# Seven products for eight in six of the eleven pairs of the last down product

## The chip, the cores and the metric

The kernel runs on one core of a Trainium2 chip. The metric is the device time of one execution in microseconds (us). Before the change it is 992.38 us, the median of three runs from 992.32 to 992.44. The core's engines are named as in the profile: PE is the matrix engine (PEld its loads of the stationary operand), DVE the vector engine, ACT the scalar engine, POOL the GpSimd engine, and SP the queue that issues the transfers from memory.

## The reference

The model has two layers on 256 tokens of width 1024, in float32. Each layer is a half-step of a gated feed-forward block, an attention, and a second such half-step; a norm closes the whole. The change touches only the last half-step of layer 1, and of that only the product with `w_down`:

```python
def swiglu(h, w_gate, w_up, w_down):
    return (jax.nn.silu(h @ w_gate) * (h @ w_up)) @ w_down

h = h + FFN_RESIDUAL_WEIGHT * swiglu(rmsnorm(h, ffn2_norm[layer]),
                                     ffn2_w_gate[layer], ffn2_w_up[layer], ffn2_w_down[layer])
...
return rmsnorm(h, final_norm)
```

The feed-forward width is 2816, so the last product multiplies act, 256 by 2816, with weights of 2816 by 1024. `FFN_RESIDUAL_WEIGHT` is 0.5.

## The kernel before

Every product in float32 is made of three matmuls in the rounded type `float32r`: each operand x is split into a high part xh (its rounding, made by ACT) and a low part xl = x - xh (made by DVE), and the product is xh wh + xh wl + xl wh. `product` (L179) issues these three matmuls for each accumulator in PSUM that it is given. The weights come in raw units of 1 MB: `unit` (L139) lets SP load one into a buffer of the ring "raw" (four buffers), and `pieces_of` (L146) splits it in pieces of 128 by 1024: ACT writes the piece's high part (L153), DVE its low part (L154). High and low parts have rings of eight buffers each, "wh" and "wl".

The last half-step runs in two stages.

**Gate and up** (`ffn_blocks`, L340). The 22 blocks f of 128 hidden columns are taken in pairs; a pair needs a raw unit of `w_gate` and one of `w_up`, eight pieces of splits in all counting both parts. `both` (L344) makes the matmuls of a block: high parts against the 512 columns of x's two parts (L193), then low parts against 256 columns (L196). `close` (L350) turns the two accumulators of a block into a block of act, with hidden columns on the partitions and the 256 tokens in the free dimension: ACT and DVE join the two halves (L336, L337), DVE scales gate (L352), ACT applies silu (L353), POOL scales up (L355), DVE multiplies (L356), and `parts_of` (L86) splits the result (ACT L94, DVE L90). All 22 blocks of act stay in SBUF.

**Last product** (`down_last`, L408). First the residual stream is transposed back to tokens on partitions (L685, L686). Then the product takes eleven units of `w_down`, each with the rows of two blocks k and all 1024 columns. For the first 18 blocks k it issues, for each of the two halves of tokens t, three matmuls for each accumulator of that half; the last four blocks are held back, and their products are issued accumulator by accumulator, so that the eviction of one (L431), the sum of squares (L698) and the final gain (L702) run beside the matmuls of the next. The accumulators are not all of one width:

```python
segs = [[(0, 0, 512), (1, 0, 512)], [(0, 0, 512), (1, 0, 256), (1, 256, 256)]]
...
if k < nk - tail:
    for t in range(NT):
        product(accs[t], *blocks[t][k], cols(t, ws), k == 0, False)
```

PSUM has eight buffers of 128 by 512: five of tag "acc" and three of tag "tr"; the last product uses the five.

Each engine works through a queue whose order is fixed when the program is built. That order is not the order of the text: the framework moves an instruction ahead of earlier ones that still wait. The profile shows splits of `w_down` (L153 on wh_f_d) on ACT at 905.55, among the closes of blocks that stand before them in the text. An instruction that writes a buffer of a ring waits until the last reader of that buffer is done.

Of the kernel before, what the change touches and what calls it, by code (L numbers as in the profile page):

```python
# [10 lines left out]
F32 = mybir.dt.float32  # L11
F32R = mybir.dt.float32r
# [3 lines left out]
P = 128  # L16
# [9 lines left out]
NG = H // HG  # L26
ROT = 16
HALF = ROT // 2
LEAD = 4
EPS = 1e-6  # L30
SCALE = DH ** -0.5
# [31 lines left out]
def trunk(ctx: ExitStack, tc: tile.TileContext, a: dict, out: bass.AP):  # L63
# [273 lines left out]
        nc.vector.tensor_add(s, ac[:, :S], s)  # L337
        return s

    def ffn_blocks(name, wg, wu, norm, first=None, beside=()):  # L340

        blocks = []

        def both(f, pair):  # L344
            acs = [acc(f"{name}_{n}{f}") for n in "gu"]
            cols = slice(f % 2 * P, (f % 2 + 1) * P)
            products_t(acs, [[(wh[:, cols], wl[:, cols]) for wh, wl in w] for w in pair], norm.x, True, True)
            return acs

        def close(f, gate, up):  # L350
            g = joined(gate, f"{name}_g{f}")
            nc.vector.tensor_mul(g, g, norm.row)  # L352
            nc.scalar.activation(g, g, AF.Silu)  # L353
            u = joined(up, f"{name}_u{f}")
            nc.gpsimd.tensor_tensor(u, u, norm.row, op=ALU.mult)  # L355
            nc.vector.tensor_mul(g, g, u)  # L356
# [48 lines left out]
        down_t(name, wd, blocks, after)  # L405


    def down_last(name, w, nk, blocks, h, weight, part, after, tail=4):  # L408


        segs = [[(0, 0, 512), (1, 0, 512)], [(0, 0, 512), (1, 0, 256), (1, 256, 256)]]
        accs = [[acc(f"dn_{name}_{t}_{c}_{o}")[:, :n] for c, o, n in segs[t]] for t in range(NT)]
        held = []

        def cols(t, ws):
            return [tuple(w[:, c * 512 + o:c * 512 + o + n] for w in ws) for c, o, n in segs[t]]

        for u in range(nk // 2):
            for i, ws in enumerate(unit(f"{name}_{u}", 2, D, [(None, rows(w, 2 * u, 2, 0, D))])):
                k = 2 * u + i  # L420
                if k < nk - tail:
                    for t in range(NT):
                        product(accs[t], *blocks[t][k], cols(t, ws), k == 0, False)
                else:
                    held.append((k, ws))
        for t in range(NT):
            for i, (c, o, n) in enumerate(segs[t]):
                for k, ws in held:
                    product(accs[t][i:i + 1], *blocks[t][k], cols(t, ws)[i:i + 1], False, k == nk - 1)
                hc = h[t][c][:, o:o + n]  # L430
                nc.vector.scalar_tensor_tensor(hc, accs[t][i], weight, hc, op0=ALU.mult, op1=ALU.add)  # L431
                part(t, slice(c * 512 + o, c * 512 + o + n))
            after(t)

    def out_t(name, pieces, base, blocks, norm, tail=3):
# [242 lines left out]
    blocks = ffn_blocks("f21", a["ffn2_w_gate"][1], a["ffn2_w_up"][1], n6)  # L678
# [25 lines left out]
    def finish(t):  # L704
# [11 lines left out]
    down_last("f21_d", a["ffn2_w_down"][1], KF,  # L716
              [[tuple(x[:, i, t * P:(t + 1) * P] for i in range(2)) for x in blocks] for t in range(NT)],
              h, 0.5, finish_part, finish)


_INS = ["ffn1_w_gate", "ffn1_w_up", "ffn1_w_down", "ffn2_w_gate", "ffn2_w_up", "ffn2_w_down",
# [23 lines left out]
```

## Time and profile before

| what | value |
| --- | --- |
| median of three runs | 992.38 us |
| the profiled execution, its own time | 992.2 us |
| its span, first to last instruction | 990.4 us |
| granted clock of PE, mean | 0.999 |
| PE busy | 979.6 us (99% of the span) |
| DVE busy | 731.3 us (74%) |
| ACT busy | 589.2 us (59%) |
| POOL busy | 163.6 us (17%) |
| gate and up of the last half-step, one pair of blocks | 11.13 us |
| last product, first to last matmul | 922.79 to 984.10 us |

In rows of the timeline the columns are start in us, length in us, engine, line, operation, output <- inputs, shapes, and the count of instructions merged in the row; brackets give the idle time of the engine before it and what ended it. Matmuls overlap, so the pace of a run of them is read from the distance of their starts. The same holds for DVE, where an instruction starts some 0.08 us before the one ahead of it is recorded as done.

### The profile page before, as it was taken

To read this page: it belongs to the slowest core of one execution; us is meant where nothing else is said; L and a number is where in the kernel's file an instruction comes from. 1 tells how busy PE (TensorE), PEld (TensorE's weight loads), DVE (VectorE), ACT (ScalarE), POOL (GpSimd) and SP (SyncE) were. 2 spreads that over 40 slices of the span, in tenths; PEclk is the share of its full clock that TensorE was granted. 3 is DMA by queue.
4 is the path that set the end of the run, shared out by engine and by line. 5 is a ranking of instruction groups with operands and counts; after the bars stand their busy time and mean duration, and the time that the engine had idled before them with its cause. 6 is when DMAs were issued, how large, how long until landed. Compare 5 with 4: busy or idle time off the path is not lost. (4 is left out here: it accounts for less than half of the span.)

```text
span 990.4 us, 15816 instructions
## 1 busy us (share of the span) xinstructions
PE 979.6 (99%) x5949; PEld 866.1 (87%) x5949; DVE 731.3 (74%) x1284; ACT 589.2 (59%) x1084; POOL 163.6 (17%) x195
## 2 busy tenths in 40 slices
PE   9999999999999999999999999999999999999997
PEld 6888888888899888888888888888889998888886
DVE  7988866667787887776678878666687778888542
ACT  6756554467776656645455666544676766655531
POOL 3211101122202211111021111111222032111000
PEclk9999999999999999999999999999999999999999
DMA  9876565654444466556646664666534445565511
GB/s 306 259 251 200 167 225 172 209 179 144 139 129 146 153 211 187 188 192 197 200 146 203 190 202 149 216 197 203 170 129 128 129 146 176 190 182 201 211 45 43
DMA packets 158398, 176.08 MB, mean 178 GB/s; under 512 B 3568, under 2 KB 152304, under 8 KB 158320
## 3 DMA queue, kind: packets, MB, share of 16 engines
q1 hardware_dynamic: 157888, 174.50, 54.8%
q8 instruction: 47, 0.77, 0.3%
q10 hardware_dynamic: 432, 0.55, 0.2%
q14 instruction: 31, 0.25, 0.1%
HBM read 173.99 MB, written 1.05 MB: 177 GB/s over the span
## 5 line engine op out<-in xcount | busy, mean ns | idle before, releaser
L193 PE MATMUL f_g<-x_n,wh_f_g 128*128 128x512 f32 x688 | 180.0, 394 | 0.0
L193 PE MATMUL f_u<-x_n,wh_f_u 128*128 128x512 f32 x688 | 177.6, 390 | 0.0
L193 PEld LDWEIGHTS f_u<-x_n,wh_f_u 128*128 128x128 f32 x688 | 129.0, 188 | 27.2
L193 PEld LDWEIGHTS f_g<-x_n,wh_f_g 128*128 128x128 f32 x688 | 124.1, 189 | 22.7
L355 POOL TENSOR_TENSOR j_f_u<-j_f_u,r_n 128x256 f32<-128x256 f32 x88 | 77.3, 880 | 378.1 <-DVE j_f_u L337 361.1
L193 PE MATMUL dn_f<-act_f,wh_f 128*128 128x512 f32 x528 | 126.5, 391 | 0.0
L154 DVE TENSOR_TENSOR wl_f_u<-raw_f_u,wh_f_u 128x1024 fp32r<-128x1024 f32 x86 | 120.8, 1406 | 1.8 <-ACT wh_f_u L153 1.7
L154 DVE TENSOR_TENSOR wl_f_g<-raw_f_g,wh_f_g 128x1024 fp32r<-128x1024 f32 x86 | 102.9, 1225 | 17.7 <-PE f_g L196 12.0
L193 PEld LDWEIGHTS dn_f<-act_f,wh_f 128*128 128x128 f32 x528 | 96.8, 188 | 18.6
L154 DVE TENSOR_TENSOR wl_f<-raw_f,wh_f 128x1024 fp32r<-128x1024 f32 x72 | 81.8, 1153 | 36.0 <-ACT wh_f L153 26.8
L196 PE MATMUL f_u<-x_n,wl_f_u 128*128 128x256 f32 x688 | 103.3, 283 | 0.0
L196 PE MATMUL f_g<-x_n,wl_f_g 128*128 128x256 f32 x688 | 102.7, 282 | 0.0
L196 PEld LDWEIGHTS f_g<-x_n,wl_f_g 128*128 128x128 f32 x688 | 96.4, 190 | 6.3
L153 ACT ACTIVATE wh_f_g<-raw_f_g 128x1024 fp32r<-128x1024 f32 x86 | 89.4, 1049 | 13.4 <-issue 6.0
L153 ACT ACTIVATE wh_f<-raw_f 128x1024 fp32r<-128x1024 f32 x72 | 67.3, 979 | 49.5 <-PE dn_f L193 30.3
L153 ACT ACTIVATE wh_f_u<-raw_f_u 128x1024 fp32r<-128x1024 f32 x86 | 86.6, 1047 | 15.7 <-PE f_g L193 10.9
L196 PEld LDWEIGHTS f_u<-x_n,wl_f_u 128*128 128x128 f32 x688 | 91.7, 192 | 0.1
L230 POOL TENSOR_TENSOR ss_n<-ss_n,sq_n 128x256 f32<-128x256 f32 x42 | 41.7, 992 | 246.5 <-ACT sq_n L229 245.6
L94 ACT ACTIVATE act_f<-j_f_g 128x256 fp32r<-128x256 f32 x88 | 36.5, 417 | 73.2 <-DVE j_f_g L356 73.1
L353 ACT ACTIVATE j_f_g<-j_f_g 128x256 f32<-128x256 f32 x88 | 36.7, 417 | 62.5 <-DVE j_f_g L352 62.1
L196 PEld LDWEIGHTS dn_f<-act_f,wl_f 128*128 128x128 f32 x528 | 68.1, 191 | 2.8
L196 PE MATMUL dn_f<-act_f,wl_f 128*128 128x256 f32 x528 | 69.0, 283 | 0.0
(213 smaller groups left out, 1798.1 us busy)
## 6 DMA issues: line engine op xcount, KB each, us to landing
raw_f_g<-in_ffn_w_gate_dram SPq DMA_DIRECT2D x43, 1024.0 KB, 5.4
raw_f_u<-in_ffn_w_up_dram SPq DMA_DIRECT2D x43, 1024.0 KB, 5.4
raw_f<-in_ffn_w_down_dram SPq DMA_DIRECT2D x24, 1024.0 KB, 5.0
raw_f_d<-in_ffn_w_down_dram SPq DMA_DIRECT2D x11, 1024.0 KB, 4.9
raw_f<-in_ffn_w_down_dram SPq DMA_DIRECT2D x12, 768.0 KB, 4.4
raw_qka<-in_a_w_qkv_dram SPq DMA_DIRECT2D x16, 512.0 KB, 4.6
raw_kvb<-in_kv_w_dram SPq DMA_DIRECT2D x12, 512.0 KB, 4.2
raw_va<-in_a_w_qkv_dram SPq DMA_DIRECT2D x4, 1024.0 KB, 5.0
```

What stands on the lines that cost most here:

```text
L94: nc.scalar.activation(hi, src, AF.Copy, scale=scale)
L153: nc.scalar.activation(wh, r, AF.Copy)
L154: nc.vector.tensor_sub(wl, r, wh.bitcast(F32))
L193: nc.tensor.matmul(ac, wh, flat(x), start=first and i == 0, stop=False)
L196: nc.tensor.matmul(ac[:, :S], wl, x[:, 0, :], start=False, stop=last and i == len(ws) - 1)
L230: nc.gpsimd.tensor_tensor(self.ss, self.ss, sq, op=ALU.add)
L353: nc.scalar.activation(g, g, AF.Silu)
L355: nc.gpsimd.tensor_tensor(u, u, norm.row, op=ALU.mult)
```

## The change

The eleven units of the last product are now called pairs 0 to 10 (two blocks k each). For the pairs in `FAST`, which are 0, 1, 3, 5, 7 and 8, the product of act's 2 by 2 quarters (token half by block) with the weights' 2 by 2 quarters (block by column half) is made in Strassen's manner, in Winograd's form: seven products of quarters where eight stood. Four sums of quarters of act and four sums of quarters of the weights are needed for it. Three products go straight into the accumulators of the results 11, 12 and 21; the other four go into accumulators m1, m5, m6 and m7 or on to 21, are added up over all six pairs, and are combined once, by `collect`, into the residual stream.

- The sums of act are made in the gate and up stage by `quarter_sums`, called from `close` of the odd block of a fast pair: four POOL instructions of 128 by 128 in a chain, then two splits of 128 by 256 (ACT and DVE). They stay in buffers that the attention used before.
- The sums of the weights are made in the last product by `load`: one DVE addition of 128 by 1024 and two POOL additions of 128 by 512 in a chain, into a second buffer of the ring "raw". A fast pair then has seven quarters to split instead of four: three pieces of 128 by 1024 and one of 128 by 512 on ACT and on DVE, in place of two of 128 by 1024.
- Pairs 2, 4 and 6 keep their eight products, the last two pairs (four blocks, as before) are held back. All accumulators are now 512 wide; the last one of the held work is cut in two halves, the second in a PSUM buffer of its own. Eight PSUM buffers are used in place of five.
- The matmuls of one accumulator are issued three in a row, where before those of two or three accumulators alternated.

```diff
+    def quarter_sums(a, b, hi, lo, name):
+        c, d = etile(f"qc_{name}"), etile(f"qd_{name}")
+        a0, a1, b0, b1 = a[:, :P], a[:, P:], b[:, :P], b[:, P:]
+        for out, x, y, op in ((c[:, :P], b1, a1, ALU.subtract), (c[:, P:], a0, a1, ALU.subtract),
+                              (d[:, :P], c[:, :P], a0, ALU.add), (d[:, P:], b0, d[:, :P], ALU.subtract)):
+            nc.gpsimd.tensor_tensor(out, x, y, op=op)
+        parts_of(hi[:, :S], lo[:, :S], c)
+        parts_of(hi[:, S:], lo[:, S:], d)
...
             parts_of(x[:, 0], x[:, 1], g)
+            if sums is not None and f // 2 in sums:
+                if f % 2 == 0:
+                    held[f // 2] = g
+                else:
+                    quarter_sums(held.pop(f // 2), g, *sums[f // 2], f"{name}_{f}")
...
+        c11, c12, c21, m1, m5 = [acc(f"dn_{name}_{n}") for n in ("11", "12", "21", "m1", "m5")]
+        c22, m6, m7 = [trt(f"dn_{name}_{n}") for n in ("22", "m6", "m7")]
...
+        def load(i):
+            raw = rawp.tile([P, 4, 512], F32, tag="raw", name=f"raw_{name}_{i}")
+            nc.sync.dma_start(raw.rearrange("p (k c) n -> p k (c n)", k=2), rows(w, 2 * i, 2, 0, D))
+            if i not in sums:
+                return split(raw[:, :2], f"{i}a") + split(raw[:, 2:], f"{i}b")
+            t = rawp.tile([P, 4, 512], F32, tag="raw", name=f"sum_{name}_{i}")
+            nc.vector.tensor_add(t[:, :2], raw[:, 0::3], raw[:, 1:2].to_broadcast([P, 2, 512]))
+            nc.gpsimd.tensor_tensor(t[:, 2], t[:, 0], raw[:, 3], op=ALU.add)
+            nc.gpsimd.tensor_tensor(t[:, 3], t[:, 2], raw[:, 2], op=ALU.add)
+            b11, b21 = split(raw[:, 0::2], f"{i}a")
+            b22, = split(raw[:, 3:], f"{i}b")
+            ta, tc = split(t[:, :2], f"{i}c")
+            tb, td = split(t[:, 2:], f"{i}d")
+            return b11, b21, b22, ta, tc, tb, td
...
+            for n, ac, left, right in (("1", m1, x[0][0], b11), ("11", c11, x[0][1], b21), ("12", c12, l3, b22),
+                                       ("5", m5, l5, ta), ("7", m7, l7, tc), ("6", m6, l6, tb),
+                                       ("21", c21, x[1][1], td)):
+                add(n, ac, left, right, last and len(n) == 1)
...
+        def collect():
+            a, b, c, d = [atile([P, 512], name=f"co_{name}_{n}") for n in "abcd"]
+            nc.scalar.activation(a, m1, AF.Copy, scale=weight)
+            nc.vector.scalar_tensor_tensor(b, m6, weight, a, op0=ALU.mult, op1=ALU.subtract)
+            nc.gpsimd.tensor_tensor(h[0][0], h[0][0], a, op=ALU.add)
+            nc.vector.scalar_tensor_tensor(c, m7, weight, b, op0=ALU.mult, op1=ALU.subtract)
+            nc.vector.scalar_tensor_tensor(b, m5, -weight, b, op0=ALU.mult, op1=ALU.add)
+            nc.gpsimd.tensor_tensor(h[0][1], h[0][1], b, op=ALU.add)
+            nc.vector.scalar_tensor_tensor(d, m5, -weight, c, op0=ALU.mult, op1=ALU.subtract)
+            nc.vector.tensor_add(h[1][0], h[1][0], c)
+            nc.vector.tensor_add(h[1][1], h[1][1], d)
...
+        pairs = KF // 2
+        ahead, held = [load(0)], []
+        for i in range(pairs):
+            if i + 1 < pairs:
+                ahead.append(load(i + 1))
+            ws = ahead.pop(0)
+            if i in sums:
+                fast(i, ws)
...
+        collect()
```

More of the change, by code (lines that the diff above doesn't have):

```diff
@@ L28 @@
 HALF = ROT // 2
+FAST = (0, 1, 3, 5, 7, 8)
 LEAD = 4
@@ L338, in joined, with ffn_blocks @@
         return s
-    def ffn_blocks(name, wg, wu, norm, first=None, beside=()):
-        blocks = []
+    def quarter_sums(a, b, hi, lo, name):
[6 more added lines that the diff above has]
+        parts_of(hi[:, S:], lo[:, S:], d)
+    def ffn_blocks(name, wg, wu, norm, first=None, beside=(), sums=None):
+        blocks, held = [], {}
         def both(f, pair):
@@ L426, in down_last @@
         for t in range(NT):
-            for i, (c, o, n) in enumerate(segs[t]):
+            for c in range(2):
+                n, ac = quarters[t][c]
+                cut = 512 if (t, c) != (1, 1) else S
                 for k, ws in held:
[L429 to L432, printed above, removed]
+                    add(n, ac[:, :cut], blocks[t][k], tuple(v[:, :cut] for v in ws[c]), k == KF - 1)
+                nc.vector.scalar_tensor_tensor(h[t][c], ac, weight, h[t][c], op0=ALU.mult, op1=ALU.add)
+                part(t, slice(c * 512, c * 512 + cut))
@@ L433, in down_last @@
+            if t:
+                for k, ws in held:
+                    add("end", end, blocks[t][k], tuple(v[:, S:] for v in ws[1]), k == KF - 1)
+                hc = h[1][1][:, S:]
+                nc.vector.scalar_tensor_tensor(hc, end, weight, hc, op0=ALU.mult, op1=ALU.add)
+                part(t, slice(512 + S, 1024))
             after(t)
@@ L677, in trunk @@
     mixer("b", segs_b, a["b_w_o"][0], masks[:, 1, :], n6)
-    blocks = ffn_blocks("f21", a["ffn2_w_gate"][1], a["ffn2_w_up"][1], n6)
+    sums = {}
+    for n, i in enumerate(FAST):
+        if n < 4:
+            parts = ap_.tile([P, 2, 512], F32R, tag=("qkh", "qkl")[n % 2], name=f"left_{i}", bufs=2)
+            sums[i] = (parts[:, 0], parts[:, 1])
+        else:
+            sums[i] = tuple(xp.tile([P, 512], F32R, tag=f"kx{4 + 2 * (n - 4) + j}", name=f"left_{i}_{j}") for j in range(2))
+    blocks = ffn_blocks("f21", a["ffn2_w_gate"][1], a["ffn2_w_up"][1], n6, sums=sums)
     h = [[xp.tile([P, 512], F32, tag=f"kx{2 * t + c}", name=f"h_{t}_{c}") for c in range(2)] for t in range(NT)]
@@ L714, in finish @@
             (nc.scalar, nc.sync)[c].dma_start(out[0, t * P:(t + 1) * P, c * 512:(c + 1) * 512], outs[t][c])
-    down_last("f21_d", a["ffn2_w_down"][1], KF,
+    down_last("f21_d", a["ffn2_w_down"][1],
               [[tuple(x[:, i, t * P:(t + 1) * P] for i in range(2)) for x in blocks] for t in range(NT)],
-              h, 0.5, finish_part, finish)
+              sums, h, 0.5, finish_part, finish)
 _INS = ["ffn1_w_gate", "ffn1_w_up", "ffn1_w_down", "ffn2_w_gate", "ffn2_w_up", "ffn2_w_down",
```

36 lines of the change are left out of this document (23 added, 13 removed).

## The prediction

> **What bounds the kernel now.** I read the page first, then the windows of the last stages, the timeline of PE in the last product, and the timeline of DVE and POOL ahead of it.
>
> ```profile
> span 990.4 us, 15816 instructions
> PE 979.6 (99%) x5949; PEld 866.1 (87%) x5949; DVE 731.3 (74%) x1284; ACT 589.2 (59%) x1084; POOL 163.6 (17%) x195
> PEclk9999999999999999999999999999999999999999
> ...
> core 0: us, PE busy (x) PEld busy (x) DVE busy (x) ACT busy (x) POOL busy (x), PEclk, DMA share, GB/s
> 911.64:922.77 11.13, 11.13 (x74) 10.05 (x73) 8.78 (x16) 7.70 (x15) 1.53 (x2) 1.00 0.53 188
> 922.77:984.10 61.33, 61.33 (x333) 52.81 (x331) 26.35 (x29) 20.00 (x28) 1.73 (x4) 1.00 0.26 95
> ```
>
> PE is busy everywhere at the full clock, and the last product (second window) is 61.33 us of PE with DVE at 26.35. Fewer matmuls there shorten the kernel one for one, as long as the others feed PE.
>
> ```profile
> 922.79 0.71 PE L182 MATMUL dn_f_d<-wh_f_d,act_f 128*128 128x512 f32 x2
> 964.68 0.64 PE L182 MATMUL dn_f_d<-wh_f_d,act_f 128*128 128x512 f32 x2
> 970.26 0.64 PE L182 MATMUL dn_f_d<-wh_f_d,act_f 128*128 128x512 f32 x2
> 973.06 0.40 PE L182 MATMUL dn_f_d<-wh_f_d,act_f 128*128 128x512 f32 x1
> 981.23 0.28 PE L182 MATMUL dn_f_d<-wh_f_d,act_f 128*128 128x256 f32 x1
> 983.98 0.28 PE L186 MATMUL dn_f_d<-wh_f_d,act_f 128*128 128x256 f32 x1
> ...
> L182 PE MATMUL dn_f_d<-wh_f_d,act_f 128*128 128x512 f32 x66 | 23.2, 396 | 0.0
> L182 PE MATMUL dn_f_d<-wh_f_d,act_f 128*128 128x256 f32 x44 | 9.3, 279 | 0.0
> ```
>
> Pace from the starts: 36 matmuls of 512 from 973.06 to 981.23 are 0.227 each; 24 of 256 from 981.23 to 984.10 (the last start plus one pace) are 0.120, more than half. Two blocks k of the mixed order, from 964.68 to 970.26, take 5.58; they are 18 of 512 and 12 of 256, which at these paces would be 18 x 0.227 + 12 x 0.120 = 5.53. So the alternating widths cost a little more.
>
> **The matmuls after.** Before: each of the three lines has 66 of 512 and 44 of 256, so 198 and 132. After: six fast pairs of 7 x 3, three plain pairs of 8 x 3, and of the held pairs 36 of 512: 126 + 72 + 36 = 234 of 512, and 24 of 256. That is 234 x 0.227 + 24 x 0.120 = 56.0 us by the rounded paces, 55.9 unrounded, against 61.3: a saving of 5.4. Of it, 18 matmuls fewer are 18 x 0.227 = 4.1; the rest is 108 halves made 54 wholes (13.0 - 12.3 = 0.7) and the mixing, 0.6. This term is sure; what can eat it is the feed.
>
> **The feed.** The low parts come from DVE, the high ones from ACT, two sums from POOL.
>
> ```profile
> 908.69 2.36 DVE L154 TENSOR_TENSOR wl_f_d<-raw_f_d,wh_f_d 128x1024 fp32r<-128x1024 f32 x2 [0.91 <-PE f_g L196]
> 910.97 0.42 DVE L337 TENSOR_TENSOR j_f_g<-f_g,j_f_g 128x256 f32<-128x256 f32 x1
> 911.30 0.41 DVE L337 TENSOR_TENSOR j_f_u<-f_u,j_f_u 128x256 f32<-128x256 f32 x1
> 911.86 0.79 POOL L355 TENSOR_TENSOR j_f_u<-j_f_u,r_n 128x256 f32<-128x256 f32 x1 [5.45 <-DVE j_f_u L337]
> 911.97 1.76 DVE L154 TENSOR_TENSOR wl_f_d<-raw_f_d,wh_f_d 128x1024 fp32r<-128x1024 f32 x1
> 913.99 1.21 DVE L154 TENSOR_TENSOR wl_f_d<-raw_f_d,wh_f_d 128x1024 fp32r<-128x1024 f32 x1
> 916.81 0.74 POOL L355 TENSOR_TENSOR j_f_u<-j_f_u,r_n 128x256 f32<-128x256 f32 x1 [4.16 <-DVE j_f_u L337]
> 917.58 0.42 DVE L356 TENSOR_TENSOR j_f_g<-j_f_g,j_f_u 128x256 f32<-128x256 f32 x1 [0.92 <-POOL j_f_u L355]
> 918.49 0.42 DVE L90 TENSOR_TENSOR act_f<-j_f_g,act_f 128x256 fp32r<-128x256 f32 x1 [0.48 <-ACT act_f L94]
> 919.83 2.36 DVE L154 TENSOR_TENSOR wl_f_d<-raw_f_d,wh_f_d 128x1024 fp32r<-128x1024 f32 x2 [0.91 <-PE f_g L196]
> ...
> L708 POOL TENSOR_TENSOR var<-var,ssq 128x1 f32<-128x1 f32 x1 | 0.2, 189 | 1.1 <-ACT sq L698 1.1
> L154 DVE TENSOR_TENSOR wl_f<-raw_f,wh_f 128x512 fp32r<-128x512 f32 x12 | 8.2, 683 | 0.0
> L153 ACT ACTIVATE wh_f_d<-raw_f_d 128x1024 fp32r<-128x1024 f32 x22 | 22.8, 1055 | 22.7 <-PE dn_f_d L186 22.7
> L153 ACT ACTIVATE wh_f<-raw_f 128x512 fp32r<-128x512 f32 x12 | 7.4, 617 | 0.0
> L431 DVE SCALAR_TENSOR_TENSOR h<-dn_f_d,h 128x512 f32<-128x512 f32 x3 | 2.1, 689 | 12.9 <-PE dn_f_d L186 12.9
> raw_f_d<-in_ffn_w_down_dram SPq DMA_DIRECT2D x11, 1024.0 KB, 4.9
> ```
>
> Back to back a DVE piece of 1024 costs 1.14 (two from 908.69 to 910.97), one of 512 about 0.60 (683 ns less the overlap of 0.08), one of 256 0.33. While POOL adds 256 columns, the DVE piece beside it takes 1.76 in place of 1.21: DVE loses 0.55. A POOL addition is 0.19 for one column and 0.74 for 256, so 1.29 for 512 and 0.46 for 128 by that slope. What DVE loses to an addition of 512 isn't shown: at least the 0.55, at most the whole 1.29; I double the row and take 1.10.
>
> *A fast pair* then costs DVE 4 x 1.14 (one addition, three splits) + 0.60 = 5.16, plus 2 x 1.10 lost to POOL: 7.36, against 7 x 3 x 0.227 = 4.76 of PE. *A plain pair* costs 2 x 1.14 = 2.28 against 5.44. ACT needs 3 x 1.06 + 0.62 = 3.8 in a fast pair, below PE. So in the fast pairs DVE and POOL together are slower than PE, and the plain pairs between them pay it back. Added up: pair 0 uses the four "wl" buffers that come free from 908.69 and is ready about when the product starts, at 922.79 (the fifth split and the sums fill what was idle). Pair 1 needs the buffers freed at 919.83 (that wait is the bracket). From there up to pair 8: five fast pairs 36.8, three plain 6.8, and the close of the last block (six DVE operations of 0.33 and 0.55 lost) 2.6: 919.83 + 46.2 = 966.1. Undisturbed, PE reaches pair 8's last piece (tb, td) at 922.79 + 6 x 4.76 + 3 x 5.44 - 2 x 0.68 = 966.3. So there is 0.2 to spare if nothing is idle. Then the held pairs' four pieces, 4.6, end at 970.6, where PE wants the last at 967.7 + 3 x 0.68 = 969.7: 0.9 late. I add 1.0 for idle moments (five fast pairs of 0.2, where the chain addition, two POOL additions, ACT, DVE isn't covered). Term: +1.9, on the path. Bounds: 0, if the plain pairs' idle DVE time all goes to work ahead; and 1.9 + 10 x 0.19 (POOL's whole 1.29) + 35 pieces x 0.08 (none overlapped) = 6.6.
>
> [...]
>
> **Sums of act, in gate and up.** Four POOL operations of 0.46 are 1.9; DVE gets two splits of 0.33 and loses about half of 0.55 four times: 1.8 in all; ACT gets two of 0.42. DVE is idle 0.92 + 0.48 + 0.91 = 2.3 in each 11.13, so it fits, and lateness has cover:
>
> ```profile
> 902.85 1.21 DVE L154 TENSOR_TENSOR wl_f_u<-raw_f_u,wh_f_u 128x1024 fp32r<-128x1024 f32 x1
> 914.54 1.12 PE L196 MATMUL f_u<-x_n,wl_f_u 128*128 128x256 f32 x8
> 922.10 0.42 DVE L337 TENSOR_TENSOR j_f_g<-f_g,j_f_g 128x256 f32<-128x256 f32 x1
> 983.98 0.28 PE L186 MATMUL dn_f_d<-wh_f_d,act_f 128*128 128x256 f32 x1
> 984.29 0.42 DVE L431 SCALAR_TENSOR_TENSOR h<-dn_f_d,h 128x256 f32<-128x256 f32 x1 [0.44 <-PE dn_f_d L186]
> 986.28 0.72 ACT L711 ACTIVATE out<-out,rms 128x512 f32<-128x512 f32 x1 [1.02 <-POOL rms L710]
> ```
>
> A piece made by 904.06 is used at 914.54. Cost 0; without that cover, up to 1.8 for each of six pairs.
>
> **What else moves.** The transfers stay eleven of 1 MB at 4.9 us; but the sums take every second raw buffer in the fast pairs, so fewer transfers run ahead (a rival below). PSUM: m1 needs the buffer of the last gate accumulator, read by 922.52, before 922.79: 0. `collect`: six DVE passes of 0.60 and two POOL additions beside the 11 us of held matmuls: 0, if DVE isn't late. The closing chain behind the last matmul (983.98 to 986.28 and on) is as before: 0.
>
> **Sum.** 992.2 (span 990.4 and 1.8 around it) - 5.4 + 1.9 = 988.7 against the profiled execution. The median of the runs is 0.2 above it, so I predict 988.9.
>
> **Rivals.**
> 1. *All hidden.* The feed never ends last, the bound 0: 992.2 + 0.2 - 5.4 = 987.0. For it: DVE is at 26 of 61 us now. Against: the 7.36 against 4.76.
> 2. *DVE and POOL bound it*: POOL's additions block DVE for their whole length and nothing overlaps. The upper bound 6.6: 992.2 + 0.2 - 5.4 + 6.6 = 993.6, break-even. For it: the 1.76 row and 0.2 to spare. Against it: only 0.55 of 0.79 is lost in that row.
> 3. *Raw buffers starve the sums* (slower). There are four; a transfer is issued as soon as one is free, and a sum needs one too, after its transfer has landed. If transfers take them first, a fast pair's sum waits until another raw buffer is used up, and its transfer and chain come one after the other: 4.9 + 1.14 + 2 x 1.29 + 1.06 + 1.21 = 10.9 for a pair that PE does in 4.76. Pairs 7 and 8 have no plain pair between: 6.2 more than the forecast, 995.1. It turns the sign once the wait passes 3.5 beyond my 1.9. Against it: two pairs of loads fit in four buffers, and pairs 2, 4, 6 need one only.
> 4. *The sums of act delay gate and up*: DVE, in its fixed order, waits for POOL's chain of four and can't use its idle time; 1.0 for each fast pair is 6.0: 994.9. Against it: 10 us of cover.
>
> **Chances.** Forecast 0.42 (987.8 to 990.4); rival 1 0.20 (986.6 to 987.8); rival 2 0.20 (990.4 to 994.4); rival 3 0.12; rival 4 0.06. A measurement of this kernel tells about 0.2% (2.0 us) from no change: faster, below 990.4, is 0.42 + 0.20 = 0.62; within 0.20; slower 0.18. The range 986.6 to 994.4 leaves out rivals 3 and 4; the likeliest's own is 987.8 to 990.4.
>
> **What would show it.** Right: PE's rows in the last product 0.227 apart in threes, 234 and 24 of them; the product some 57.8 us long; DVE without gaps there; its pieces beside POOL's additions longer by about 1.1; gate and up still 11.13 a pair. Wrong: idle PE before pairs 7, 8 or the held work released by DVE over 4 us in all; a sum's addition waiting on a raw buffer; pairs of gate and up longer than 11.13.

## The result, and the profile after

The kernel became slower: 999.19 us, the median of six runs (998.68 to 999.72), against 992.31 us of the kernel before on the same chip (992.23 to 992.44). The ratio is 1.0069, with a 95% interval from 1.0056 to 1.0082. The prediction was 988.9 us with a range from 986.6 to 994.4, so both the sign and the range were wrong.

In the profile after, line numbers are shifted: the matmuls of gate and up are L194 and L197 (L193 and L196 before), the three matmuls of `product` are L183, L185 and L187, the close's L336, L337, L352, L353, L355 and L356 are L337, L338, L365, L366, L368 and L369, its splits L94 and L90 are L95 and L91, and the transposed h is L774 and L775. New are the additions on POOL in `quarter_sums` (L347), the splits of these sums (on `left`, by L95 and L91 too), and in the last product the splits L441 (ACT) and L442 (DVE) and the sums of weights (L451 on DVE, L452 and L453 on POOL).

The page of the kernel after begins thus:

```profile
span 997.4 us, 15783 instructions
PE 978.3 (98%) x5877; PEld 862.8 (87%) x5877; DVE 770.0 (77%) x1320; ACT 601.6 (60%) x1109; POOL 209.9 (21%) x233
PEclk9999999999999999999999999999999999999899
```

PE has 72 instructions fewer and yet was busy only 1.3 us less, in a span 7.0 us longer. One slice of the granted clock shows an 8, where before all 40 showed a 9. The windows of stages say where. The columns are the window, its length, then busy time of PE, PEld, DVE, ACT and POOL with the number of instructions in brackets, the granted clock, the share of DMA and GB/s. First the kernel before, in two windows:

```profile
814.90:904.38 89.48, 89.48 (x518) 79.10 (x518) 73.37 (x121) 55.58 (x102) 15.59 (x18) 1.00 0.60 189
904.38:922.79 18.41, 18.41 (x114) 16.39 (x113) 13.72 (x25) 13.28 (x24) 2.27 (x3) 1.00 0.49 172
```

And the kernel after, the same two windows and two later ones:

```profile
814.90:904.38 89.48, 89.48 (x518) 79.10 (x518) 75.10 (x123) 55.54 (x107) 29.71 (x39) 1.00 0.53 165
904.38:922.79 18.41, 15.58 (x77) 13.00 (x76) 16.92 (x23) 8.26 (x18) 9.55 (x10) 0.91 0.16 58
922.77:933.33 10.56, 5.47 (x39) 4.98 (x38) 8.09 (x14) 7.24 (x15) 1.30 (x2) 0.85 0.59 199
933.33:991.04 57.71, 57.71 (x260) 48.04 (x258) 52.00 (x50) 30.35 (x40) 24.03 (x13) 0.97 0.40 137
```

Up to 904.38 PE does the very same work at the same pace: 518 matmuls in 89.48 us in both. Then come two windows in which PE is idle and its clock is lower. The last product begins at 933.33 instead of 922.79, 10.5 us late, and takes 57.7 us instead of 61.3, with PE busy from end to end. So 10.5 - 3.6 = 6.9 us of the 7.0 are found. The delays arose ahead of the product, in gate and up and in the transposes behind them; what the product itself lost, 1.8 us against the 55.9 predicted, comes from the lower clock behind them (below).

The list of what PE waited for, summed over the run, has two entries at its head which the kernel before doesn't have (columns: total us, how often, the longest):

```profile
PE h L774 <- ACT h L775: 5.1, 1, 5.1
PE f_u L194 <- DVE j_f_g L338: 2.8, 2, 1.9
```

They can be placed by PE's own timeline:

```profile
903.42 1.12 PE L197 MATMUL f_u<-x_n,wl_f_u 128*128 128x256 f32 x8
904.38 2.00 PE L194 MATMUL f_g<-x_n,wh_f_g 128*128 128x512 f32 x8
908.24 2.65 PE L194 MATMUL f_u<-x_n,wh_f_u 128*128 128x512 f32 x8 [1.86 <-DVE j_f_g L338]
...
913.62 1.99 PE L194 MATMUL f_g<-x_n,wh_f_g 128*128 128x512 f32 x8
...
922.14 2.12 PE L194 MATMUL f_u<-x_n,wh_f_u 128*128 128x512 f32 x8 [0.97 <-DVE j_f_g L338]
...
932.56 1.12 PE L774 MATMUL h<-ident,hT 128*128 128x128 f32 x4 [5.09 <-ACT h L775]
933.33 0.78 PE L183 MATMUL dn_f_d_m<-wh_f_d_0a,act_f 128*128 128x512 f32 x1
933.90 0.63 PE L185 MATMUL dn_f_d_m<-wl_f_d_0a,act_f 128*128 128x512 f32 x1
934.33 0.63 PE L187 MATMUL dn_f_d_m<-wh_f_d_0a,act_f 128*128 128x512 f32 x1
```

The block that begins at 904.38 takes 9.24 us instead of 5.57, the last block 6.83, and the transposes 7.3 instead of 1.7. Both waits in the blocks are of the first matmul into the accumulator of "up", and what ends them is the DVE instruction of an earlier block's close that reads the accumulator of "gate" for the last time. The kernel has five such buffers in PSUM, a block takes two, so block 19's "up" takes the buffer of block 17's "gate". Block 17 ends on PE one block before 904.54, at 898.97; block 19 wants the buffer at 904.38 + 8 x 0.227 = 906.20. **A close has 7.2 us from the end of its block to the point at which PE stands still.** That is the cover that counts, and the prediction did not look at it.

How late the closes were is read from ACT: the start of the instruction that opens a close (L336 before, L337 after, on the gate accumulator) less the end of the block's last matmul. A negative number means that it ran while "up" was still being made.

| block | 4 | 8 | 12 | 16 | 17 | 18 | 19 | 20 | 21 |
| --- | --- | --- | --- | --- | --- | --- | --- | --- | --- |
| before, us | 1.2 | -0.5 | -0.9 | -0.9 | 0.0 | -0.9 | 0.0 | -0.9 | 0.0 |
| after, us | 3.1 | 5.0 | 5.4 | 5.8 | 6.1 | 9.4 | 5.9 | 5.8 | 5.2 |

So the closes were three to six microseconds late in most blocks, for 90 us, and PE did not show it as long as 7.2 us covered them. Then a little more made it show. ACT's timeline of the kernel before has a close that waits only for PE:

```profile
903.66 0.38 ACT L336 ACTIVATE j_f_g<-f_g 128x256 f32<-128x256 f32 x1 [0.28 <-PE f_g L196]
```

ACT's timeline after:

```profile
905.04 0.36 ACT L337 ACTIVATE j_f_g<-f_g 128x256 f32<-128x256 f32 x1
...
910.89 0.42 ACT L95 ACTIVATE act_f<-j_f_g 128x256 fp32r<-128x256 f32 x1 [1.60 <-DVE j_f_g L369]
912.35 0.42 ACT L95 ACTIVATE left<-qc_f 128x256 fp32r<-128x256 f32 x1 [1.04 <-POOL qc_f L347]
913.57 0.42 ACT L95 ACTIVATE left<-qd_f 128x256 fp32r<-128x256 f32 x1 [0.81 <-POOL qd_f L347]
913.90 0.36 ACT L337 ACTIVATE j_f_g<-f_g 128x256 f32<-128x256 f32 x1
...
930.45 1.04 ACT L441 ACTIVATE wh_f_d_1d<-sum_f_d 128x1024 fp32r<-128x1024 f32 x1
931.39 0.36 ACT L337 ACTIVATE j_f_g<-f_g 128x256 f32<-128x256 f32 x1
931.92 1.08 ACT L775 ACTIVATE h<-h 128x512 f32<-128x512 f32 x2
```

ACT works in its fixed order, and the close of block 18 (913.90) stands behind the splits of block 17's sums (912.35, 913.57), which wait for POOL. ACT is idle there for 1.9 us that end with POOL and 1.6 that end with DVE, while a full accumulator waits to be read. At the end the copies of h (931.92), which PE's transposes wait for, stand behind the last close, and that stands behind the splits of pair 1.

DVE's timeline beside it shows why the close that began at 905.04 was done only at 908.18:

```profile
904.14 3.70 DVE L155 TENSOR_TENSOR wl_f_g<-raw_f_g,wh_f_g 128x1024 fp32r<-128x1024 f32 x2
907.77 0.41 DVE L338 TENSOR_TENSOR j_f_g<-f_g,j_f_g 128x256 f32<-128x256 f32 x1
```

and POOL's timeline of the same stretch:

```profile
902.58 1.36 POOL L452 TENSOR_TENSOR sum_f_d<-sum_f_d,raw_f_d 128x512 f32<-128x512 f32 x1 [1.22 <-DVE sum_f_d L451]
904.02 1.35 POOL L453 TENSOR_TENSOR sum_f_d<-sum_f_d,raw_f_d 128x512 f32<-128x512 f32 x1
905.34 1.43 POOL L347 TENSOR_TENSOR qc_f<-j_f_g 128x128 f32<-128x128 f32 x1
...
910.94 1.37 POOL L347 TENSOR_TENSOR qc_f<-j_f_g,j_f_g 128x128 f32<-128x128 f32 x1 [1.49 <-DVE j_f_g L369]
```

Two DVE pieces, which took 2.36 with POOL idle (the kernel before, 908.69), took 3.70 here. And POOL's additions of 128 columns, 0.52 and 0.55 at the end of the same chain (912.39 and 912.99), took 1.37 and 1.43 beside DVE's pieces. In these rows each engine slows the other.

**The lower clock.** The matmuls behind each idle stretch do not run at the pace of 0.227: the eight from 908.24 start 0.305 apart in the mean, the eight from 922.14 0.244, those of the product 0.43 from 933.90 to 936.89, and the window of the product has a granted clock of 0.97. Of the 12.3 us lost (10.5 of start and 1.8 in the product), PE's idle time is 8.3 (2.04 + 1.15, counted from when the next matmul was due, and the 5.1 of the transposes); the other 4.0 are matmuls at the slow pace behind it: 1.6 in the block from 904.38, 0.1 in the last block, 0.5 in the transposes, 1.8 in the product. The slow stretch behind the longest wait goes from 932.56 to 936.89, 4.3 us.

### The profile page after: what moved, and what is told of

Same layout as the page of the kernel before. It is cut to its first block, busy times and chain, and to the rows that moved or that the text cites. A ratio compares the mean times of both kernels' runs of the same rounds, so it can differ in the third digit from the quotient of the medians.

```text
span 997.4 us, 15783 instructions
## 1 busy us (share of the span) xinstructions
PE 978.3 (98%) x5877; PEld 862.8 (87%) x5877; DVE 770.0 (77%) x1320; ACT 601.6 (60%) x1109; POOL 209.9 (21%) x233
## 5 line engine op out<-in xcount | busy, mean ns | idle before, releaser
L194 PE MATMUL f_u<-x_n,wh_f_u 128*128 128x512 f32 x688 | 178.4, 391 | 2.8 <-DVE j_f_g L338 2.8
L194 PE MATMUL f_g<-x_n,wh_f_g 128*128 128x512 f32 x688 | 180.0, 393 | 0.0
L194 PEld LDWEIGHTS f_u<-x_n,wh_f_u 128*128 128x128 f32 x688 | 129.0, 188 | 30.8 <-DVE j_f_g L338 3.7
L368 POOL TENSOR_TENSOR j_f_u<-j_f_u,r_n 128x256 f32<-128x256 f32 x88 | 78.5, 894 | 350.0 <-DVE j_f_u L338 332.9
L194 PEld LDWEIGHTS f_g<-x_n,wh_f_g 128*128 128x128 f32 x688 | 124.1, 189 | 22.7
L194 PE MATMUL dn_f<-act_f,wh_f 128*128 128x512 f32 x528 | 126.5, 391 | 0.0
L194 PEld LDWEIGHTS dn_f<-act_f,wh_f 128*128 128x128 f32 x528 | 96.8, 188 | 18.6
L197 PE MATMUL f_u<-x_n,wl_f_u 128*128 128x256 f32 x688 | 103.6, 283 | 0.0
L197 PE MATMUL f_g<-x_n,wl_f_g 128*128 128x256 f32 x688 | 103.5, 284 | 0.0
L197 PEld LDWEIGHTS f_g<-x_n,wl_f_g 128*128 128x128 f32 x688 | 97.2, 192 | 6.4
L197 PEld LDWEIGHTS f_u<-x_n,wl_f_u 128*128 128x128 f32 x688 | 92.0, 192 | 0.1
L95 ACT ACTIVATE act_f<-j_f_g 128x256 fp32r<-128x256 f32 x88 | 36.4, 416 | 73.7 <-DVE j_f_g L369 73.6
L366 ACT ACTIVATE j_f_g<-j_f_g 128x256 f32<-128x256 f32 x88 | 36.7, 417 | 66.4 <-DVE j_f_g L365 66.0
L197 PEld LDWEIGHTS dn_f<-act_f,wl_f 128*128 128x128 f32 x528 | 68.1, 191 | 2.8
L197 PE MATMUL dn_f<-act_f,wl_f 128*128 128x256 f32 x528 | 69.0, 283 | 0.0
```

The source lines that it names most:

```text
L95: nc.scalar.activation(hi, src, AF.Copy, scale=scale)
L194: nc.tensor.matmul(ac, wh, flat(x), start=first and i == 0, stop=False)
L197: nc.tensor.matmul(ac[:, :S], wl, x[:, 0, :], start=False, stop=last and i == len(ws) - 1)
```

## The experiments

Two theories were left by the traces. **A**: DVE and POOL slow or even exclude one another, so each addition on POOL takes time from DVE (and the other way), and closes come late. **B**: the fixed order of the engines waits for POOL's slow chains, whoever is to blame for their length. A third, the prediction's own, was that the feed of the last product is too slow. All ratios are against the kernel before, on the same chip.

### Leaving out the sums of act

```diff
-                    quarter_sums(held.pop(f // 2), g, *sums[f // 2], f"{name}_{f}")
+                    held.pop(f // 2)
...
-            l5, l7, l6, l3 = [tuple(v[:, j * P:(j + 1) * P] for v in sums[i]) for j in range(4)]
+            l5, l7, l6, l3 = x[1][0], x[1][1], x[0][1], x[1][0]
```

> Left out: the four sums of quarters of act and their splits in the gate and up stage; the fast pairs take plain quarters of act as left factors instead, so the matmuls stay as many. Before, the last product starts at 922.79; in the changed kernel at 933.33, 10.5 us late, and is itself 3.6 shorter. Theory A (the sums of act, POOL's chain and the DVE splits behind it, put the closes of gate and up a block behind): the start goes back to 922.8 to 925 and the time is 986.8 to 989.5. Theory B (the weight sums and larger splits of pairs 0 and 1, done ahead in the last two pairs of gate and up, cause it): the start stays at 929 or later and the time is 994 or more.

Measured: 992.44 (991.76 to 993.13), ratio 1.0000 (0.9990 to 1.0009). The closes are as punctual as before up to block 16, then 1.3 to 4.7 us late in the last five blocks, where POOL's first sums of weights fall. Gate and up end at 921.34 without an idle moment; only the transposes wait, as PE's timeline shows:

```profile
921.34 1.47 PE L773 MATMUL h<-ident,hT 128*128 128x128 f32 x12
926.45 0.66 PE L773 MATMUL h<-ident,hT 128*128 128x128 f32 x4 [3.64 <-ACT h L774]
```

The start, 926.86, and the time lie between what the two theories said. So the sums of act, which the prediction put at 0, cost 6.8 us with their splits (999.19 - 992.44). The rest of the loss is still there without them.

### Leaving out the sums of weights

```diff
-            t = rawp.tile([P, 4, 512], F32, tag="raw", name=f"sum_{name}_{i}")
-            nc.vector.tensor_add(t[:, :2], raw[:, 0::3], raw[:, 1:2].to_broadcast([P, 2, 512]))
-            nc.gpsimd.tensor_tensor(t[:, 2], t[:, 0], raw[:, 3], op=ALU.add)
-            nc.gpsimd.tensor_tensor(t[:, 3], t[:, 2], raw[:, 2], op=ALU.add)
...
-            ta, tc = split(t[:, :2], f"{i}c")
-            tb, td = split(t[:, 2:], f"{i}d")
+            ta, tc = split(raw[:, :2], f"{i}c")
+            tb, td = split(raw[:, 2:], f"{i}d")
```

> Left out: the sums of quarters of the weights (one DVE and two POOL additions for each fast pair and the second raw buffer); the quarters themselves are split a second time, so splits and matmuls stay as many. Theory A (sums of act): the closes still lag by 3 to 6 us through gate and up and the last product starts at 927 or later, time 992 to 996. Theory B (work of pairs 0 and 1 ahead): the start goes back to 922.8 to 925, time 986.8 to 989.5. If both are needed, both this and the kernel without the sums of act are near 988.

Measured: 993.73 (993.51 to 994.97), ratio 1.0017 (1.0007 to 1.0026). Product from 928.43; the transposes wait 4.4 us for ACT's copies of h, and a block of gate and up 0.3 us for its accumulator. So with either kind of sum alone the transposes are late, and the two together cost more than either. No run leaves out both kinds and keeps the splits; whether ACT's seven quarters for a fast pair, in place of four, would do it by themselves is open.

### No fast pair at all

```diff
-FAST = (0, 1, 3, 5, 7, 8)
+FAST = ()
```

with `collect` left out where there are no sums.

> No fast pair at all, eight products everywhere; what stays of the change is the order of three matmuls in a row for each accumulator, and 512 wide accumulators with one cut at the end. By the paces of the trace of before (0.227 for 512, 0.120 for 256) the last product is 1.3 us shorter: 991.0. If the pace of 0.227 came from the idle DVE and ACT at the end and not from the order, no change: 992.3.

Measured: 991.24 (991.15 to 991.62), ratio 0.9989 (0.9979 to 0.9998). The product's matmuls, from first to last start, take 59.99 us instead of 61.19, and begin at 922.99. This is the part of the saving that has nothing to do with Strassen: wholes for halves, and no mixing of widths. The prediction had 0.7 + 0.6 = 1.3 for it; 1.2 was measured.

### All sums on DVE

```diff
-            nc.gpsimd.tensor_tensor(out, x, y, op=op)
+            nc.vector.tensor_tensor(out, x, y, op=op)
...
-            nc.gpsimd.tensor_tensor(t[:, 2], t[:, 0], raw[:, 3], op=ALU.add)
-            nc.gpsimd.tensor_tensor(t[:, 3], t[:, 2], raw[:, 2], op=ALU.add)
+            nc.vector.tensor_tensor(t[:, 2], t[:, 0], raw[:, 3], op=ALU.add)
+            nc.vector.tensor_tensor(t[:, 3], t[:, 2], raw[:, 2], op=ALU.add)
```

> All sums, of act and of weights, made by DVE in place of POOL; all else as in the changed kernel. A POOL addition of 512 beside DVE costs DVE 1.10 (2.31 in place of 1.21), on DVE itself 0.60. If the exclusion of DVE and POOL is what makes the closes late, DVE gains 1.0 for each fast pair in the last product and the waits of the chains go: start at 923 to 926, time 987 to 991. If it is the amount of DVE work and its fixed order alone, the start stays at 930 or later and the time above 995.

Measured: 991.98 (990.25 to 993.40), ratio 0.9994 (0.9984 to 1.0003). DVE gets all of these sums, and the kernel is 7.2 us faster than the change, though its median lies 1 us above the 987 to 991 of the first theory. The closes are 0.5 to 2.5 us late in most blocks, and PE loses nothing in gate and up. In the profiled execution, which took 990.46, the product starts at 926.33 and takes 56.0 us, which is the 55.9 of the prediction. Eight of the ten executions took 991.81 to 993.40 with a granted clock of 0.996 to 0.997, where this one had 0.999. What is left is the transposes, which wait 3.1 us, for the last close still stands on ACT behind pair 1:

```profile
923.80 1.04 ACT L441 ACTIVATE wh_f_d_1d<-sum_f_d 128x1024 fp32r<-128x1024 f32 x1
924.74 0.36 ACT L337 ACTIVATE j_f_g<-f_g 128x256 f32<-128x256 f32 x1
```

### Three fast pairs, away from the start

```diff
-FAST = (0, 1, 3, 5, 7, 8)
+FAST = (2, 4, 6)
```

The sums stay on POOL.

> Fast pairs 2, 4 and 6 alone, sums on POOL as in the changed kernel: no fast pair among the first two, whose loads fall into the end of gate and up, and none among the last four of gate and up's own pairs. Matmuls saved: 9 x 0.227 = 2.0, and 1.2 for the order of the matmuls (measured with no fast pair). If the loss sits where gate and up passes into the last product, the start is 922.8 to 923.5 and the time 989.0 to 990. If the sums of act put every close behind wherever they stand, the start is 925 or later and the time above 992.

Measured: 995.82 (995.00 to 996.41), ratio 1.0034 (1.0022 to 1.0046). Gate and up run without an idle moment, but the product starts at 927.84, since the transposes wait 4.3 us. The closes are 3.7 to 4.9 us late in the last three blocks: pair 2's four pieces are split on ACT ahead of the last close even though pairs 0 and 1 are plain. Half the sums bring half the loss (3.4 us against 6.9); moving them away from the start does not remove it.

### The transposes moved away from the end

If the transposes only show a lateness that lies elsewhere, then moving them must not help. They depend on nothing in gate and up, so they can be issued in the first blocks:

```diff
+    def stream(t):
+        for c in range(2):
+            tr = trt(f"h_{t}_{c}")
+            for k in range(4):
+                nc.tensor.transpose(tr[:, k * P:(k + 1) * P], hT[:, 4 * c + k, t * P:(t + 1) * P], ident)
+            nc.scalar.activation(h[t][c], tr, AF.Copy)
...
+    blocks = ffn_blocks(..., sums=sums, beside=[None, lambda: stream(0), lambda: stream(1)])
```

First in the change as it is, with the sums on POOL:

> The changed kernel with the early transposes alone, sums on POOL. Its transposes waited 5.1 us of the 10.5 that the start is late. If they are a cause, 5 us are won: 993.5 to 994.5. If they only show how late the closes are, PE waits in the product's first matmuls for the accumulators of the last block instead, 1 to 2 us are won: 997 to 998.5.

Measured: 1000.10 (999.91 to 1000.12), ratio 1.0077 (1.0063 to 1.0091). Nothing is gained, not even the 1 to 2 us of the second theory: the wait moves into the product. The list of PE's waits now begins:

```profile
PE dn_f_d_m L183 <- DVE j_f_g L338: 3.9, 1, 3.9
PE f_u L194 <- DVE j_f_g L338: 2.2, 2, 1.4
```

The matmul that waits is the first into m5, and what ends the wait is the instruction of the last close that reads the accumulator of "gate": m5 takes the buffer of the last block's gate.

Then with all sums on DVE:

> All sums on DVE, and the transposes of the residual stream, with ACT's copies, moved from the end of gate and up to its second and third pair. With the sums on DVE alone the last product was 55.9 long, as predicted, but started 3.5 late, since a fourth transpose waited for ACT's copies, which stand behind the splits of pair 1. If that wait is a matter of place alone, it goes, the product starts near 923 and the time is 987.0 to 988.0. If the wait only passes on to the next thing that is late (the accumulators of the last block, freed at 925.6 to 926.8), the start or the fourth product waits and the time is 989 to 990.5.

Measured: 989.30 (989.19 to 991.19), ratio 0.9976 (0.9966 to 0.9986): faster than the kernel before, and in the range of the second theory. The product begins at 922.99. One wait is left, the same as above but 1.9 us long. Here moving the transposes does help, by 2.7 us (991.98 to 989.30).

Then with the sums of act on DVE and only the sums of weights on POOL:

> Sums of act on DVE, sums of weights on POOL as in the changed kernel, early transposes. Tells the two places of POOL's additions apart. If POOL beside DVE hurts in gate and up alone, this is near the kernel with all sums on DVE: 987 to 989. If the weight sums' 1.10 for each POOL addition starves the product once it starts on time (7.36 for each fast pair against 4.76 on PE, by the prediction 1.9 of waiting), 989 to 991.

Measured: 997.53 (997.49 to 997.79), ratio 1.0052 (1.0037 to 1.0068). Both theories were far too low. Two additions on POOL in each of six pairs, against the same two on DVE, make 8.2 us. Compared with the version before, the product begins 0.6 us later (923.59), is 5.7 us longer from first to last start (63.71 against 58.00), and the span ends 8.4 us behind the last start instead of 6.4. Of the 5.7, 2.0 are a longer wait at m5 (3.9 instead of 1.9) and 0.5 a wait for a low part of pair 10; the matmuls behind the wait at m5 start 0.43 apart up to 935.57. DVE has twelve additions less to do and is busy 774.5 us instead of 769.4.

This trace also shows theory B. Pair 3's first addition on POOL took 3.89 us, where those of the change at 902.58 and 904.02 took 1.36; the rows of POOL, ACT and DVE behind it:

```profile
938.26 3.89 POOL L452 TENSOR_TENSOR sum_f_d<-sum_f_d,raw_f_d 128x512 f32<-128x512 f32 x1 [5.47 <-DVE sum_f_d L451]
943.55 1.06 ACT L441 ACTIVATE wh_f_d_3d<-sum_f_d 128x1024 fp32r<-128x1024 f32 x1 [4.25 <-POOL sum_f_d L453]
944.64 1.23 DVE L442 TENSOR_TENSOR wl_f_d_3d<-sum_f_d,wh_f_d_3d 128x1024 fp32r<-128x1024 f32 x1 [3.64 <-ACT wh_f_d_3d L441]
```

### Additions on POOL that nobody needs

This tests theory A without POOL's chain of sums. To the version that took 989.3, with all sums on DVE, four additions of 256 columns on POOL are added in each fast pair, into a buffer that nothing reads (lines of the last product are numbered one higher here):

```diff
+            for k in range(4):
+                nc.gpsimd.tensor_tensor(spare, t[:, k // 2, :S], raw[:, 3, k % 2 * S:][:, :S], op=ALU.add)
```

> All sums on DVE and the transposes of h early, as in the version that took 989.3; added are four additions of 256 columns on POOL in each fast pair (24 in all), of operands that are there anyway, into a buffer that nothing reads. Nothing waits for them, but they keep POOL as busy as the two sums of 512 of the change would (4 x 0.74 = 3.0 against 2 x 1.36 = 2.7). Theory A, the time goes because DVE cannot run beside POOL: DVE loses about 0.55 to each, 24 x 0.55 = 13 us, and it had 5 us left of 66 in the last product and the block before it, so 8 us more: about 997. Theory B, the time goes because the engines' fixed order waits for POOL's slow chain of two sums: nobody waits here, so 989.3 to 990.5.

Measured: 1002.08 (1001.71 to 1002.20), ratio 1.0095 (1.0081 to 1.0109); 12.8 us more than without them. DVE's timeline in the product without them:

```profile
951.69 1.22 DVE L451 TENSOR_TENSOR sum_f_d<-raw_f_d 128x1024 f32<-128x1024 f32 x1
...
953.96 0.68 DVE L452 TENSOR_TENSOR sum_f_d<-sum_f_d,raw_f_d 128x512 f32<-128x512 f32 x1
```

and with them, DVE's timeline and then POOL's group of additions (x24, busy us, mean ns):

```profile
947.17 1.76 DVE L443 TENSOR_TENSOR wl_f_d_4b<-raw_f_d,wh_f_d_4b 128x1024 fp32r<-128x1024 f32 x1
949.56 1.23 DVE L452 TENSOR_TENSOR sum_f_d<-raw_f_d 128x1024 f32<-128x1024 f32 x1 [0.63 <-POOL spare_f_d L456]
...
951.84 1.23 DVE L453 TENSOR_TENSOR sum_f_d<-sum_f_d,raw_f_d 128x512 f32<-128x512 f32 x1
```

```profile
L456 POOL TENSOR_TENSOR spare_f_d<-sum_f_d,raw_f_d 128x256 f32<-128x256 f32 x24 | 33.2, 1382 | 19.4 <-DVE sum_f_d L452 15.7 <-issue 2.4
```

A piece of 512 takes 1.23 instead of 0.68, one of 1024 takes 1.76 instead of 1.22: 0.54 lost to each addition of 256, and POOL's addition takes 1.38 instead of 0.74 (the kernel before, L355 at 905.68). What theory A says of the time is shown (whether the two engines exclude one another is not): work on POOL whose result nobody uses costs more than the sums did, and DVE is busy 780.6 us instead of 769.4 with the same 1356 instructions, 11.2 us more. Theory A's number, 997, was too low by 5. Not all of the 12.8 us need be DVE's loss, for it is not quite true that nobody waits: the additions also hold raw buffers (the 0.63 in the second row) and stand in POOL's queue ahead of the closes' L368. PE waits 5.3 us for accumulators (1.9 without the additions) and 2.7 us for low parts of pairs 8 and 10, the end of the span lies 8.4 us behind the last start instead of 6.4, and behind the 3.8 us of idle at m5 the matmuls start 0.43 apart again, from 932.12 to 936.38. How much of this DVE's loss alone would bring was not told apart. Theory B is not refuted as a second cause: in the timeline of the change and in the one above ACT does wait, in order, for POOL's chain.

### The first pair plain

With the sums on DVE and the transposes early, what is left is the 1.9 us at m5. A plain pair needs neither m1 nor m5:

```diff
-FAST = (0, 1, 3, 5, 7, 8)
+FAST = (1, 2, 4, 5, 7, 8)
```

> All sums on DVE, the transposes of h early, and six fast pairs again, but 1, 2, 4, 5, 7 and 8, so that the product begins with a plain pair. Theory, the 1.9 us that PE waited in pair 0 (989.3) is the accumulator m5, which stands in the bank that the close of the last gate block frees too late: a plain pair needs three of the five banks and not m5, so the wait goes, and the two slow matmuls behind it: 987.0. Rival, the lateness lies with DVE, which carries 6 x 6.4 + 5 x 2.3 us: two pairs of neighbours starve PE and it stays at 989 or above.

Measured: 988.29 (988.03 to 988.42), ratio 0.9957 (0.9944 to 0.9969). The window of the product has no idle PE:

```profile
923.19:979.24 56.05, 56.05 (x260) 46.75 (x258) 54.27 (x64) 30.36 (x41) 7.07 (x6) 1.00 0.41 149
```

The wait is gone and 2.2 us with it in the product (58.00 to 55.82 from first to last start). But the time went down by 1.0 only, to between what theory and rival said: the span ends 7.5 us after the last start of a matmul, where it was 6.4 before and in the version of 989.3. DVE, busy 54.27 of 56.05, comes late to `collect` and to the last evictions.

With four fast pairs:

```diff
+FAST = (2, 4, 6, 8)
```

> As the last, with four fast pairs, 2, 4, 6 and 8, each with a plain pair before it. Six matmuls more than with six fast pairs, 6 x 0.227 = 1.4 us. Theory: the wait in pair 0 goes (2.2 less than 989.3), 1.4 comes back: 988.4. If it is as fast as the one with six, the six were still bound by DVE; if it is above 989.3, the wait was not the accumulator.

Measured: 988.53 (988.50 to 988.60), ratio 0.9959 (0.9946 to 0.9973). Six matmuls more, and the same time: the two fast pairs more were worth 1.4 us of PE and lost about 1.1 of it at the end.

With five fast pairs, the last of them pair 7, so that `collect` can begin a pair earlier:

```diff
+FAST = (1, 2, 4, 5, 7)
```

> As the version with pairs 1, 2, 4, 5, 7 and 8 (988.29), without pair 8: three matmuls more, 0.68 us of PE, and 5 us less for DVE. Theory: in that version PE never waits, but DVE comes 1.1 us late to the last eviction, because collect and the evictions stand behind its backlog (the span ends 7.3 us after the last matmul instead of 6.4); with less for DVE the 1.1 go and the 0.68 come: 987.9. Rival: the end is late by POOL's two additions in collect, which stay; then 0.68 more, 989.0.

Measured: 987.80 (987.71 to 987.95), ratio 0.9953 (0.9939 to 0.9966). The product is 0.68 longer (56.50), the end is 6.4 us after the last start again. The rival's 989.0 is out. Fewer splits and sums for DVE and an earlier `collect` changed together here; but with four fast pairs, the last of them still pair 8, the end is 6.4 us too, so DVE's load is the likelier of the two. This is the fastest of all: 4.6 us below the kernel before, 11.4 below the change.

## Why the prediction was wrong

**The matmuls after: right.** 55.9 us were predicted for the product, called sure. Where the granted clock of the product's window is 1.00 and PE is never idle in it, it takes 56.0 (sums on DVE; six fast pairs with a plain first pair). In the change 57.7 were measured, and the 1.8 on top are the slow pace at its start. That 57.7 nearly meets the 57.8 which the prediction named as a sign of being right (55.9 and 1.9 of feed) is chance, for no feed is in it.

**The feed: the mechanism right, the place wrong.** A DVE piece beside an addition of 512 on POOL was put at 1.10 longer. In the change it takes 2.31 to 2.33 instead of 1.21, so 1.10; the doubling had been an assumption, and it came out:

```profile
938.18 1.22 DVE L442 TENSOR_TENSOR wl_f_d_2a<-raw_f_d,wh_f_d_2a 128x1024 fp32r<-128x1024 f32 x1
939.32 2.33 DVE L442 TENSOR_TENSOR wl_f_d_2b<-raw_f_d,wh_f_d_2b 128x1024 fp32r<-128x1024 f32 x1
```

But the term +1.9 "on the path" did not occur: PE was never idle in the product of the change. That is no proof of the plain pairs' slack, for the product began 10.5 us late and DVE had that time for work ahead. In the two versions with early transposes and the weights' sums on POOL, whose products begin 7.2 and 9.7 us earlier, the term shows itself: PE waited 0.4 and 0.5 us for a low part of pair 10, and the span ended 8.4 us behind the last start instead of 6.4, since DVE came late to `collect` and the evictions. That is 2.4 and 2.5 us, near the 1.9, but part of it sits in the closing chain, where the prediction had 0, and PE's wait of 3.9 us at m5 had given DVE time. What the feed costs with no such wait no run shows.

The most that DVE could lose to 512 columns, POOL's whole 1.29, was the author's estimate, and it was not reached: 1.10 to 512 columns and 0.54 to 256 were measured. That POOL's additions take longer beside DVE as well was left out of the prediction's sum. By the rows what POOL loses is of a similar size: 2.16 instead of 1.36 for 512 columns, 1.38 instead of 0.74 for 256.

**Sums of act, in gate and up: this is the step that failed.** "Cost 0", it said, since a weight piece is made 10 us before its use. That cover is real and PE never waited for a weight piece in gate and up. But the piece is not what a late DVE or ACT hurts first. The close frees an accumulator, and its cover is 7.2 us. The step added up busy time (1.8 us against 2.3 idle) where it should have followed the order: the split of a sum stands on ACT ahead of the next block's close and waits for POOL's four additions, of which two took 1.4 us and two 0.53 in the last chain (0.46 each were predicted). The sign that the prediction had named for it was there: the last two pairs of gate and up took 14.81 and 12.38 us instead of 11.13. Without the sums of act the kernel took 992.44, 6.8 us less than with them. That a waiting instruction holds back what is queued behind it was applied to DVE alone, in rival 4, at 6.0 us, and dismissed with the 10 us of cover at a chance of 0.06. Rival 4 is what happened, with ACT as the engine that waits, and the 6.8 is near its 6.0. The rest, up to 999.19, is in the terms that follow: without the sums of act the time was still 3.5 us above the forecast.

**The additions on POOL count twice.** The first sums of the weights (pairs 0 and 1) run not in the product but in the last blocks of gate and up. The feed was costed from 922.79 on, as if only the product had to pay. Without the sums of act the transposes still wait 3.6 us. That is not POOL's doing alone: with all sums on DVE they wait 3.1, because the splits of pair 1 stand on ACT ahead of the last close in both.

**PSUM: wrong.** "m1 needs the buffer of the last gate accumulator, read by 922.52: 0." The time of the read was taken from the trace of before. When the closes are late, that buffer is too, and it is m5, not m1, that takes it and shows it: 3.9 us with the sums on POOL, 1.9 with them on DVE. In the change as it is the wait is hidden behind the longer one of the transposes.

**The transposes were not mentioned at all.** ACT's copies of h stand behind the last close and so inherited its lateness, 5.1 us, the largest single wait.

**The clock: missing.** PE's idle time was costed at its length. In the profiled execution it cost about half as much again: 8.3 us of idle brought 4.0 us of slow matmuls.

**Collect and the closing chain: 0, with the right condition.** "If DVE isn't late", it said. Where DVE was late (six fast pairs, sums on DVE) they cost 1.1 us, and five fast pairs won them back; with the weights' sums on POOL and early transposes they cost 2.0.

**Rival 3, raw buffers,** did not decide: PE was never idle in the product of the change. As with the feed, the late start makes that a weak test.

## What to carry to other kernels

Before an idle engine is given work, look at what stands behind the new wait in each engine's order, and at the shortest cover among all that it delays; here the accumulators' 7.2 us and not the weights' 10. A stage can run late for a long time without PE showing it, so compare the distance between a producer's end and its consumer's start, not only idle PE. And POOL was no free helper of a busy DVE here: an addition that cost DVE 0.60 to do cost it 1.10 to be spared.

## What the runs showed of the hardware

- Additions on POOL and the additions and subtractions on DVE beside them both took longer: with 24 additions of 256 columns on POOL that nobody reads the kernel took 12.8 us more, with 0.54 lost by a DVE instruction to an addition beside it, 11.2 us more of busy DVE in all, and 1.38 instead of 0.74 for an addition on POOL.
- In the traces of the change, of the version without sums of act, of the change with early transposes and of the version with additions that nobody needs PE was idle for 5.1, 3.6, 3.9 and 3.8 us, and for 4.3, 3.8, 6.1 and 4.9 us behind that it was slow, with matmuls of 512 columns 0.43 apart instead of 0.227. Behind 3.1 us of idle, in the execution of 990.46 with all sums on DVE, only one distance, 0.32, is longer. After 1.9 us of idle it varied: in the change the block from 904.38 lost 1.6 us to slow matmuls, and the version with early transposes and all sums on DVE has five executions at 989.2 to 989.3 with a granted clock of 0.998 to 0.999, and four at 990.8 to 991.2 with 0.996 to 0.997. With its wait removed, all five executions lie within 0.4 us.
- Once PE doesn't wait, seven products for eight brought what their matmuls are worth: five fast pairs against none brought 991.24 - 987.80 = 3.4 us, and 15 matmuls fewer are 15 x 0.227 = 3.4.
